# A fused encoder block on one core: the input's second half loaded behind row tile 1, modulation in two operations, the time steps inside the indexer, the feed-forward weight sums inside the top-k search

## The chip, the core and the metric

The kernel runs as one program on one core of one Trainium2 chip. The metric is the device time of one execution in microseconds (us). The engines are called PE (TensorE, matrix products; PEld is its weight load), DVE (VectorE), ACT (ScalarE), POOL (GpSimd) and SP (SyncE, which here only issues DMAs). Each engine works through its own list of instructions in order, and waits where the next instruction's inputs or buffers are not ready.

## The reference

One layer of a streaming encoder, over 1024 positions of width 1024, all in float32:

```python
mod = (silu(c) @ ada_w + ada_b)              # shift_m, scale_m, gate_m, shift_f, scale_f, gate_f
h = rmsnorm(x, pre_norm_mix) * (1 + scale_m) + shift_m
proj = h @ w_in      # q_lat, kv_lat, k_idx, w_idx, z, xbc, dt_raw, g_a, g_b
y_a = sparse_mla_attention(...) @ w_o_attn   # indexer scores -> top 256 keys per query -> attention
y_b = ssd_mixer(z, xbc, dt_raw, ...) @ w_o_ssd   # causal conv, dt = softplus(dt_raw + dt_bias), scan, silu(z) gate
mix = (sigmoid(g_a) * y_a + sigmoid(g_b) * y_b) @ w_out
x = x + gate_m * rmsnorm(mix, post_norm_mix)
h2 = rmsnorm(x, pre_norm_ffn) * (1 + scale_f) + shift_f
u_gate, u_up = split(h2 @ w_ffn_in)
x = x + gate_f * rmsnorm((silu(u_gate) * u_up) @ w_ffn_out, post_norm_ffn)
```

## The kernel before, in words

Activations lie transposed: 128 channels on the partitions, positions along the row, in two halves `b` = 0, 1 of 512 positions. The 1024 input channels are eight row tiles `k` of 128. Every float32 product is made of three PE products: each operand is split into a rounded part `hi` and a rest `lo`, and hi·hi, hi·lo and lo·hi are summed in PSUM.

**The head** (lines 345 to 501) makes `h`. PE's, ACT's and DVE's lists follow the written order there (`in_order`). For each row tile, `k_load` starts three DMAs on SP (the 192 KB piece `p1raw` of the first projection weight and two 512 KB pieces `ada` of the modulation weight), `k_ada` multiplies `ada` with the conditioning vector, `k_mod` finishes `amul` and `mod` (one scale and one shift per channel) and splits `p1raw`, `k_x` multiplies the half row tile by the spread reciprocal root `rx`, `k_h` makes `h`'s `hi` on ACT and `lo`, and `k_mm` runs its nine matmuls of 512 columns into the banks `pp`. `x_squares` and `rstd` make the norm's sums. The second half of `x` is eight DMAs of 256 KB from `x_load(1)`.

**The stages behind the head.** After `h` comes a run of wide projections: `wide` streams one 128-column tile of `w_in` and multiplies it with both halves of `h`, 48 matmuls, first into the bank of `b` = 0 and then that of `b` = 1, alternating over two pieces of four row tiles. These `pw` banks have three buffers in rotation (`bank_d`). Streamed weights are split by `whi` on ACT (L158) and `wlo` on POOL (L159). The fill list is

```python
FILL = "xxxxx" + "z" * 16 + "a" * 8
```

that is five conv groups of four tiles (evacuated by ACT and nine DVE operations, L1002 to L1004), sixteen `z` gates and eight `a` gates (evacuated by one ACT operation per bank, `g` at L992).

**What the fill stands beside.** The indexer makes scores with PE, ACT and DVE (`acc`, L667). Then the top-k search runs: two groups of rows in 32 dependent steps each. Group `v` counts on DVE (L715), group `s` counts on ACT (L717); both do their bookkeeping in DVE operations of 3 columns (L724 to L728, L757 to L760). ACT's list mixes the counts of `s` with the `g` evacuations of the fill. The time steps `dt` (`dt_part`, L567) are a chain of some seventeen DVE operations on 128x256 with a few small matmuls. `weight_sums` (L1022) makes sums and differences of blocks of `w_ffn_out`: in each of 12 units four loads, four POOL operations, four stores to the DRAM tile `d_t`, which the feed-forward output reads much later.

**What sets the order.** Outside the head a scheduler that walks its own timeline orders each engine's list when the program is built, bound by data, by buffers in rotation and by the `behind` dependences that the code adds. The order stays fixed when the program runs.

Of the kernel before, what the change touches and what calls it, by code (L numbers as in the profile page):

```python
# [17 lines left out]
P = 128  # L18
# [51 lines left out]
def build(tc, a, dbg=None, stop=99, slots=None):  # L70
# [23 lines left out]
    def f(x):  # L94
        return x.bitcast(F32)
# [251 lines left out]
    def x_load(b, after):  # L347
        for k in range(KT):
            t = Q(f"x{k}")
            tc.add_manual_dep(SP.dma_start(t, a["xT"][k][:, half(b)]).ins, after, mybir.DependencyInfo(  # L350
                mybir.DependencyClass.NoSync, mybir.DependencyReason.DATA), reason="behind")
            X0[k][b] = t

    def x_squares(b, ks, sums):
        for k in ks:
# [30 lines left out]
        first[k] = split(Q, raw, "p1", (P, 3, P), lo_eng=G)  # L386

    def k_x(k, b):
        V.tensor_tensor(X0[k][b], X0[k][b], rx[b], op=OP.mult)

    def k_h(k, b):
        x = X0[k][b]
        hi, lo = HB[b][k]
        i1 = S.activation(hi, x, AF.Identity, bias=mod[:, k:k + 1], scale=amul[:, k:k + 1])
        V.tensor_scalar(x, x, amul[:, k:k + 1], mod[:, k:k + 1], op0=OP.mult, op1=OP.add)
        i2 = (G if b and k > 1 else V).tensor_tensor(lo, x, f(hi), op=OP.subtract)
        if k == 7:
            barrier.update((i.ins.engine, i.ins.name) for i in (i1, i2))
        Hs[k][0][b], Hs[k][1][b] = hi, lo
        dump("h", x, (k, slice(None), half(b)))  # L400

    HB = [[(H_(f"h{k}h", dt=F32R), H_(f"h{k}l", dt=F32R)) for k in range(KT)] for b in BS]

# [15 lines left out]
    with in_order(*ORDERED):  # L419
        p = bank_d("warm")  # L420
        for i in range(WARM):
            T.matmul(p, ones, ones[:, None, :].to_broadcast([P, 4, P]), start=i == 0, stop=i == WARM - 1)
        sums = [None, None], [None, None]
        x_squares(0, range(2), sums[0])
        i = k_load(0, X0[1][0]).ins
        for k in (1, 2, 3):
            i = k_load(k, after=i.name).ins
        x_load(1, i.name)
        x_squares(0, range(2, 8), sums[0])
        r0 = rstd(sums[0], D)  # L430
        k_ada(0)
        pr0 = rspread(r0)
        k_mod(0)
        rx[0] = Q("rx")
        S.activation(rx[0], pr0, AF.Copy)
        pp1 = [[(bank if t or b else bank_d)(f"pp{t}") for b in BS] for t in range(3)]
        k_x(0, 0)
        k_h(0, 0)
        k_ada(1)
        k_x(1, 0)  # L440
        k_mm(0, 0, [0])
        k_mod(1)
        k_h(1, 0)
        k_mm(0, 0, [1, 2])
        k_ada(2)
        k_x(2, 0)
        k_mm(1, 0, [0])
        k_mod(2)
        k_h(2, 0)
        x_squares(1, range(2), sums[1])  # L450
        k_mm(1, 0, [1, 2])
        k_ada(3)
        k_x(3, 0)
        k_mm(2, 0, [0])
        k_mod(3)
        x_squares(1, range(2, 4), sums[1])
        k_h(3, 0)
        k_mm(2, 0, [1, 2])
        k_x(4, 0)
        x_squares(1, range(4, 8), sums[1])  # L460
        k_mm(3, 0, [0])
        k_load(4)
        k_ada(4)
        k_mm(3, 0, [1, 2])
        k_mod(4)
        k_h(4, 0)
        r1 = rstd(sums[1], D)
        k_mm(4, 0, [0, 1])
        pr1 = rspread(r1)
        rx[1] = Q("rx")  # L470
        S.activation(rx[1], pr1, AF.Copy)
        k_x(0, 1)
        k_h(0, 1)
        k_mm(4, 0, [2])
        i = k_load(5).ins
        barrier[i.engine] = i.name
        k_ada(5)
        k_x(1, 1)
        k_h(1, 1)
        k_x(2, 1)  # L480
        k_mm(0, 1)
        for k in range(5, KT):
            if k > 5:
                i = k_load(k).ins
                barrier[i.engine] = i.name
                k_ada(k)
            k_x(k, 0)
            k_mm(k - 4, 1, [0])
            k_mod(k)
            k_h(k, 0)  # L490
            k_mm(k - 4, 1, [1, 2])
            k_h(k - 3, 1)
            k_x(k - 2, 1)
            k_mm(k, 0)
        for k in range(5, KT):
            k_h(k, 1)
            if k + 1 < KT:
                k_x(k + 1, 1)
            k_mm(k - 1, 1)
        k_mm(KT - 1, 1)  # L500
        const_loads()
    if stop <= 0:
        ctx.close()
# [49 lines left out]
    kept = steady()  # L553
    dt, acum, decay, cdec = consts(kept)
    widx = kept[:, 896:1024].rearrange("p (t h) -> p t h", t=NT)
    tmp = [R("dt_tmp", (P, 4, NT, 32)) for _ in range(2)]
    xd, e, q, pl = (tmp[0][:, i] for i in range(4))
    dA = tmp[1][:, 0]
    for b in BS:
        pt = bank("pmt")  # L560
        for t in range(4):
# [5 lines left out]
    def dt_part():  # L567
        S.activation(e, xd, AF.Abs)
        i = S.activation(e, e, AF.Exp, scale=-1.0).ins.name
        nA = con.tile([P, 32], F32, name="nA")  # L570
        tc.add_manual_dep(S.activation(nA, alb, AF.Exp).ins, i, mybir.DependencyInfo(
            mybir.DependencyClass.NoSync, mybir.DependencyReason.DATA), reason="behind")
        V.tensor_scalar(q, e, 2.0, None, op0=OP.add)
        V.reciprocal(q, q)
        V.tensor_tensor(q, e, q, op=OP.mult)
        V.tensor_tensor(e, q, q, op=OP.mult)
        V.tensor_scalar(pl, e, 1.0 / 17.0, None, op0=OP.mult)
        for m in (15, 13, 11, 9, 7, 5, 3):
            V.scalar_tensor_tensor(pl, pl, 1.0 / m, e, op0=OP.add, op1=OP.mult)
# [12 lines left out]
        V.tensor_copy(acum.rearrange("p t h -> p (t h)"), pc[:, 0:256])
        tot = tmp[1][:, 1, 0:NCH, :]
        V.tensor_copy(tot.rearrange("p c h -> p (c h)"), ptot[:, 0:128])
        V.tensor_tensor(decay.rearrange("p (c t) h -> p c t h", t=2), tot[:, :, None, :].to_broadcast([P, NCH, 2, 32]),
                        acum.rearrange("p (c t) h -> p c t h", t=2), op=OP.subtract)
        S.activation(decay, decay, AF.Exp)
        S.activation(cdec, tot, AF.Exp)
        acT = [R("acT") for b in BS]
        for b in BS:  # L600
            pa = bank("pacT")
            for t in range(4):
                T.transpose(pa[0:32, t * P:(t + 1) * P], acum[:, 4 * b + t, :], ident)
            for dst, fn in ((d_ac, AF.Copy), (d_ea, AF.Exp)):
                t = acT[b][0:32, 512 * (fn == AF.Exp):512 * (fn == AF.Exp) + 512]
                S.activation(t, pa[0:32], fn)
                SP.dma_start(dst[2 * b:2 * b + 2].rearrange("c h l -> h c l"), t.rearrange("h (c l) -> h c l", c=2))
        dump("dt", dt)
        dump("acum", acum)
        SP.dma_start(d_kept, kept[:, 0:896])  # L610

    dt_part()


    bt = R("btmp", (P, 1024))
# [399 lines left out]
    KH = FT // 2  # L1015
    d_t = dr.tile([4, 4, P, KH, P], F32, name="d_t")
    units = iter([(c, k0) for c in range(4) for k0 in (0, 4, 8)])
    sum_bufs = [wp.tile([P, 4, P], F32, name="adaw", tag="adaw", bufs=2) for _ in range(2)]
    both = vp.tile([P, NT, P], F32, name="vt", bufs=1)
    sum_bufs += [both[:, 0:4], both[:, 4:8]]  # L1020

    def weight_sums(c, k0):  # L1022

        n = min(4, KH - k0)
        b11, b12, b21, b22 = (x[:, 0:n] for x in sum_bufs)
        for x, t, o in ((b11, c, 0), (b12, 4 + c, 0), (b22, 4 + c, KH), (b21, c, KH)):
# [41 lines left out]
    def conv_group(g):  # L1068
        for t in group_tiles(g):
            conv_out(conv(*t))  # L1070
            if g > 1:
                weight_sums(*next(units))

    pend = []

# [62 lines left out]
    for kind in FILL:  # L1138
        if kind == "x":
            conv_group(next(n_x))  # L1140
        elif kind == "z":
            t = next(n_z)
            gate(1 + t, d_z[t], AF.Silu)
            if t == 3:
                ada_after = [W.issue]
            if t == 12:
                rows.append(ada_rows())
        else:
            t = next(n_a)
            gate(49 + t, d_sga[t], AF.Tanh, 0.5)  # L1150
# [1084 lines left out]
```

## Time and profile before

| | |
|---|---|
| median of 3 runs | 2319.97 us (2319.41 to 2320.04) |
| profiled execution | 2321.74 us, of it the span from first to last instruction 2319.8 us |
| mean granted PE clock | 0.994 of full speed |
| PE busy | 2293.4 us, 99% of the span |
| DVE, ACT, POOL busy | 71%, 52%, 38% |
| DMA, mean over the span | 178 GB/s |

A matmul row shows its start, its duration and, in brackets, the idle time of its engine just ahead of it with what ended that idle time. Matmuls are pipelined: a row's duration is longer than the step to the next row (0.227 us at full clock, 0.427 us at half). In a group row the columns are line, engine, operation, output and inputs with shapes and count, then busy time, mean ns of one, and idle time ahead of the group. In a table of windows each engine has its busy time and the number of its instructions, then come the granted PE clock, the share of the 16 DMA engines in use, and GB/s.

### The profile page before, as it was taken

The numbers are of one execution on the slowest core, as the hardware profiler recorded it, in microseconds if no ns is written. First come the engines' busy times: TensorE is split into PE (matmuls) and PEld (weight loads), VectorE is DVE, ScalarE is ACT, GpSimd is POOL, SyncE is SP. The second block draws the span as 40 slices with busy tenths as digits, with TensorE's granted clock in tenths as the row PEclk, the third lists the DMA queues.
The fourth block names the chain that finished last, engine by engine and source line by source line (L and its number), as shares of the span: only waits on it lengthen the run. The fifth ranks groups of instructions, "written<-read, shape, count | busy, mean of one in ns | idle before, by whom it ended". The sixth has DMA issues, their size and how long they took to land. (4 is left out here: it accounts for less than half of the span.)

```text
span 2319.8 us, 34896 instructions
## 1 busy us (share of the span) xinstructions
PE 2293.4 (99%) x11672; PEld 1880.2 (81%) x11672; DVE 1650.2 (71%) x3249; ACT 1216.7 (52%) x2355; POOL 883.8 (38%) x691
## 2 busy tenths in 40 slices
PE   8999999999999999999999999999999999999997
PEld 5778888888888888888788788888788888888886
DVE  5466887399587777766567879685778776646675
ACT  4346666476635555556767666444555222235442
POOL 1434651222253334333335443100122555444556
PEclk8999999999999999999999999999999999999999
DMA  7137552522244444433679889674573444438664
GB/s 275 58 115 250 202 178 89 164 100 96 96 127 156 155 142 153 146 117 127 202 258 302 279 281 318 226 232 145 180 247 127 153 161 155 150 109 284 201 195 164
DMA packets 252147, 412.70 MB, mean 178 GB/s; under 512 B 25616, under 2 KB 93376, under 8 KB 251968
## 3 DMA queue, kind: packets, MB, share of 16 engines
q1 hardware_dynamic: 238720, 388.93, 50.8%
q10 hardware_dynamic: 13248, 21.56, 3.1%
q8 instruction: 92, 1.51, 0.3%
q14 instruction: 87, 0.71, 0.1%
HBM read 305.83 MB, written 107.70 MB: 178 GB/s over the span
## 5 line engine op out<-in xcount | busy, mean ns | idle before, releaser
L159 POOL TENSOR_TENSOR wlo<-wraw,whi 128x512 fp32r<-128x512 f32 x152 | 210.7, 1387 | 383.8 <-ACT whi L158 345.1
L1793 PE MATMUL p<-xh,wr 128*128 128x512 f32 x880 | 271.9, 389 | 0.0
L158 ACT ACTIVATE whi<-wraw 128x512 fp32r<-128x512 f32 x238 | 149.1, 628 | 204.7 <-issue 61.3
L1793 PEld LDWEIGHTS p<-xh,wr 128*128 128x128 f32 x880 | 165.2, 188 | 34.2
L1793 PE MATMUL p<-xl,wr 128*128 128x512 f32 x440 | 171.2, 389 | 0.0
L1787 POOL TENSOR_TENSOR wr<-a,wr 128x512 fp32r<-128x512 f32 x82 | 115.8, 1421 | 133.6 <-ACT wr L1786 100.0
L256 POOL TENSOR_TENSOR fwl<-fw,fwh 128x512 fp32r<-128x512 f32 (+1 forms) x78 | 106.3, 1371 | 103.9 <-ACT fwh L255 75.8
L872 ACT ACTIVATE lg<-lg,mx 128x256 f32<-128x256 f32 (+7 forms) x128 | 98.9, 773 | 74.8 <-DVE mx L869 74.1
L1786 ACT ACTIVATE wr<-a 128x512 fp32r<-128x512 f32 x107 | 66.7, 629 | 127.7 <-PE p L1793 89.5
L274 POOL TENSOR_TENSOR r<-v,nhalf 128x4 f32<-128x4 f32 (+1 forms) x17 | 25.4, 1497 | 255.1 <-DVE v L272 251.9
L667 DVE SCALAR_TENSOR_TENSOR acc<-rel,steady,acc 128x384 f32<-128x384 f32 (+2 forms) x90 | 103.1, 1175 | 13.6 <-ACT rel L662 13.5
L1793 PE MATMUL p<-h2h,wr 128*128 128x512 f32 x352 | 110.0, 390 | 0.0
L717 ACT ACTIVATE junk<-acc,cand__2214 128x1024 bf16<-128x1024 f32 (+2 forms) x96 | 86.2, 898 | 39.1 <-DVE cand__2214 L760 27.0
L662 ACT ACTIVATE rel<-prel 128x512 f32<-128x512 f32 (+3 forms) x160 | 77.2, 522 | 38.2 <-PE prel L661 36.6
L1793 PEld LDWEIGHTS p<-xl,wr 128*128 128x128 f32 x440 | 82.6, 188 | 17.2
L715 DVE TENSOR_SCALAR_CACHE_REDUCE junk<-acc,cand__2223 128x896 bf16<-128x896 f32 (+2 forms) x96 | 88.5, 922 | 1.4
L1717 PE MATMUL pos<-yh,wlo 128*128 128x512 f32 x224 | 87.8, 392 | 1.3 <-DVE wlo L159 1.3
L1717 PE MATMUL pos<-yh,whi 128*128 128x512 f32 x224 | 87.8, 392 | 0.0
L1717 PE MATMUL pos<-yw,whi 128*128 128x512 f32 x224 | 87.2, 390 | 0.0
L1787 POOL TENSOR_TENSOR wr<-s,wr 128x512 fp32r<-128x512 f32 x40 | 55.9, 1398 | 76.8 <-ACT wr L1786 69.5
L159 DVE TENSOR_TENSOR wlo<-wraw,whi 128x512 fp32r<-128x512 f32 x86 | 60.2, 701 | 34.1 <-ACT whi L158 33.9
L893 PE MATMUL pt<-ident,lg 128*128 128x128 f32 x576 | 82.8, 273 | 0.2 <-ACT lg L872 0.2
(691 smaller groups left out, 7279.0 us busy)
## 6 DMA issues: line engine op xcount, KB each, us to landing
wraw<-w_in SPq DMA_DIRECT2D x129, 256.0 KB, 2.7
a<-w_ffn_in SPq DMA_DIRECT2D x122, 256.0 KB, 3.3
al<-d_a SPq DMA_DIRECT2D x88, 256.0 KB, 4.2
yl<-d_y SPq DMA_DIRECT2D x72, 256.0 KB, 5.1
adaw<-ada_t SPq DMA_DIRECT2D x64, 256.0 KB, 2.7
al<-d_ac SPq DMA_DIRECT2D x32, 512.0 KB, 5.6
d_a<-g SPq DMA_DIRECT2D x42, 256.0 KB, 2.3
ada<-ada_p SPq DMA_DIRECT2D x16, 512.0 KB, 7.9
```

What stands on the lines that cost most here:

```text
L158: self.hi = behind(S.activation(hi[:, :kt], raw[:, :kt], AF.Copy))
L159: self.lo = behind(self.eng[len(self.tiles) % len(self.eng)].tensor_tensor(lo[:, :kt], raw[:, :kt], f(hi[:, :kt]), op=OP.subtract))
L256: (lo_eng or V).tensor_tensor(lo, src, f(hi), op=OP.subtract)
L662: S.activation(rel[:, 512 * b:512 * b + w_], pr[:, 0:w_], AF.Relu)
L667: V.scalar_tensor_tensor(acc[i][:, 0:n], rel[:, 0:n], ws, acc[i][:, 0:n], op0=OP.mult, op1=OP.add)
L715: V.tensor_scalar(jk, y, a_, 0.0, op0=op, op1=OP.add, accum_out=o)
L717: S.activation(jk, y, AF.Sign, scale=-1.0, bias=a_, accum_out=o)
L872: S.activation(lg[:, 0:n], lg[:, 0:n], AF.Exp, scale=-1.0, bias=m, accum_out=rr[:, 2 * t + hh:2 * t + hh + 1])
L893: T.transpose(ptv[:, hh, t, :], PR[hh, t][:, j * P:(j + 1) * P], ident)
L1717: T.matmul(p, w[k // 4][wi][:, k % 4], YO[i][k][xi], start=start and k == 0 and n == 0, stop=k == SK - 1 and n == 2, skip_group_check=True)
L1787: parts_last[0] = parts_eng[0].tensor_tensor(w[:, 1], src, f(w[:, 0]), op=OP.subtract).ins.name
L1793: T.matmul(p, w[:, wi, i], X[x][i][xi], start=start and i == 0 and k == 0, stop=i == 3 and k == 2, skip_group_check=True)
```

## The change

The change has four parts.

1. In the head, `x_load(1)` is issued behind the DMAs of row tile 1, not behind those of row tile 3; the loads of row tiles 4 to 7 are issued by a helper `k_more`; and the written order changes: the second half's squares and `rstd` come earlier, and from row tile 3 on both halves of a row tile are multiplied directly one after the other.
2. The modulation takes two operations behind `rx`: `k_x` multiplies by `amul` and `rx` in one DVE operation, ACT's `hi` then only adds `mod`, and `lo` is one DVE operation, (x + mod) - hi, for both halves. The DVE operation at L395 is gone, and POOL makes no `lo` of `h` any more.
3. `dt_part()` is called in the first `z` gate of the fill and not ahead of the indexer. Its temporaries lie in other buffers.
4. `weight_sums` is called in the `z` gates 4 to 15, one unit each, and not in the last three conv groups.

```diff
-        V.tensor_tensor(X0[k][b], X0[k][b], rx[b], op=OP.mult)
+        V.scalar_tensor_tensor(X0[k][b], X0[k][b], amul[:, k:k + 1], rx[b], op0=OP.mult, op1=OP.mult)
...
-        i1 = S.activation(hi, x, AF.Identity, bias=mod[:, k:k + 1], scale=amul[:, k:k + 1])
-        V.tensor_scalar(x, x, amul[:, k:k + 1], mod[:, k:k + 1], op0=OP.mult, op1=OP.add)
-        i2 = (G if b and k > 1 else V).tensor_tensor(lo, x, f(hi), op=OP.subtract)
+        i1 = S.activation(hi, x, AF.Identity, bias=m)
+        i2 = V.scalar_tensor_tensor(lo, x, m, f(hi), op0=OP.add, op1=OP.subtract)
...
-        for k in (1, 2, 3):
-            i = k_load(k, after=i.name).ins
-        x_load(1, i.name)
+        i = k_load(1, after=i.name).ins
+        i = x_load(1, i.name)
+        for k in (2, 3):
+            i = k_load(k, after=i).ins.name
...
+        for k in range(3, KT):
+            more = k + 1 < KT
+            if more:
+                k_ada(k + 1)
+            k_mm(k, 0, [0])
+            if more:
+                k_mod(k + 1)
+            k_mm(k, 0, [1, 2])
+            if more:
+                for b in BS:
+                    k_x(k + 1, b)
+                for b in BS:
+                    k_h(k + 1, b)
+            k_mm(k, 1)
...
-    dt_part()
...
             conv_out(conv(*t))
-            if g > 1:
-                weight_sums(*next(units))
...
             t = next(n_z)
+            if t == 0:
+                dt_part()
             gate(1 + t, d_z[t], AF.Silu)
+            if t > 3:
+                weight_sums(*next(units))
```

How the lists move is seen at three places. In the rows below a row has its line, the operation, output and inputs, the shape, and a count where it stands several times in a row; lines behind 350 have other numbers in the changed kernel.

SP's list at its start, before: `ada` are the modulation weights of one row tile, `x` with 128x512 the second half of the input.

```order
L368 DMA p1raw<-w_p 128x384
L373 DMA ada_198<-ada_p 128x1024
L373 DMA ada_199<-ada_p 128x1024
L368 DMA p1raw<-w_p 128x384
L373 DMA ada_204<-ada_p 128x1024
L373 DMA ada_205<-ada_p 128x1024
L368 DMA p1raw<-w_p 128x384
L373 DMA ada_210<-ada_p 128x1024
L373 DMA ada_211<-ada_p 128x1024
L350 DMA x_215<-xT 128x512
L350 DMA x_217<-xT 128x512
```

The same piece of SP's list in the changed kernel, from the weights of row tile 1 on:

```order
L375 DMA ada_198<-ada_p 128x1024
L375 DMA ada_199<-ada_p 128x1024
L350 DMA x_203<-xT 128x512
L350 DMA x_205<-xT 128x512
L350 DMA x_207<-xT 128x512
L350 DMA x_209<-xT 128x512
L350 DMA x_211<-xT 128x512
L350 DMA x_213<-xT 128x512
L350 DMA x_215<-xT 128x512
L350 DMA x_217<-xT 128x512
L370 DMA p1raw<-w_p 128x384
L375 DMA ada_220<-ada_p 128x1024
```

The eight `x` DMAs now stand ahead of the weights of row tiles 2 and 3.

DVE's list around the `dt` chain, before: `dt_tmp` are the chain's temporaries, `cv` with `pw` a conv tile's evacuation.

```order
L574 RECIPROCAL dt_tmp<-dt_tmp 128x256
L1002 SCALAR_TENSOR_TENSOR cv<-pw,vec,cv 128x511
L575 TENSOR_TENSOR dt_tmp<-dt_tmp 128x256
L576 TENSOR_TENSOR dt_tmp<-dt_tmp 128x256
L577 TENSOR_SCALAR dt_tmp<-dt_tmp 128x256
L579 SCALAR_TENSOR_TENSOR dt_tmp<-dt_tmp 128x256 x5
L1003 SCALAR_TENSOR_TENSOR cv<-pw,vec,cv 128x1
L1004 SCALAR_TENSOR_TENSOR cv<-pw,vec,cv 128x511
```

DVE's list around the chain in the changed kernel: `qs` and `acc` belong to the indexer.

```order
L642 TENSOR_TENSOR qs<-pqi,qs 64x256
L571 TENSOR_SCALAR dt_tmp<-dt_tmp 128x256
L572 RECIPROCAL dt_tmp<-dt_tmp 128x256
L998 SCALAR_TENSOR_TENSOR cv<-pw,vec,cv 128x1
L999 SCALAR_TENSOR_TENSOR cv<-pw,vec,cv 128x511
L997 SCALAR_TENSOR_TENSOR cv<-pw,vec,cv 128x510
L573 TENSOR_TENSOR dt_tmp<-dt_tmp 128x256
L998 SCALAR_TENSOR_TENSOR cv<-pw,vec,cv 128x2
L999 SCALAR_TENSOR_TENSOR cv<-pw,vec,cv 128x510
L642 TENSOR_TENSOR qs<-pqi,qs 64x512
```

The chain now begins behind the indexer's first rows and stands more thinly among the conv rows; it still is ahead of the search.

POOL's list from the last norm of the head to the end of the search, before: `wlo` is the split of a streamed weight, `nm` the first work of the attention.

```order
L274 TENSOR_TENSOR r<-v,nhalf 128x4
L256 TENSOR_TENSOR kvtl<-lat,kvth 128x512
L159 TENSOR_TENSOR wlo<-wraw,whi 128x512
L256 TENSOR_TENSOR kvtl<-lat,kvth 128x512
L159 TENSOR_TENSOR wlo<-wraw,whi 128x512 x41
L819 TENSOR_TENSOR nm<-nb,dmask 128x2x128
```

POOL's list within the search in the changed kernel: `adaw` and `vt` are the buffers of the weight sums (buffer numbers shown).

```order
L159 TENSOR_TENSOR wlo_4677<-wraw_4675,whi_4676 128x512
L1029 TENSOR_TENSOR vt_4735<-vt_4735 128x512
L159 TENSOR_TENSOR wlo_4754<-wraw_4752,whi_4753 128x512
L1026 TENSOR_TENSOR adaw_4736<-adaw_4737,adaw_4736 128x384
L1027 TENSOR_TENSOR adaw_4737<-vt_4735,adaw_4737 128x384
L1028 TENSOR_TENSOR vt_4735<-vt_4735,adaw_4736 128x384
L1029 TENSOR_TENSOR vt_4735<-vt_4735 128x384
L159 TENSOR_TENSOR wlo_4760<-wraw_4758,whi_4759 128x512
L159 TENSOR_TENSOR wlo_4834<-wraw_4832,whi_4833 128x512
L1026 TENSOR_TENSOR adaw_4736<-adaw_4737,adaw_4736 128x512
```

Where only `wlo` stood, each two `wlo` now have four sums beside them, in twelve units over the fill tiles `z` 4 to 15.

More of the change, by code (lines that the diff above doesn't have):

```diff
@@ L352, in x_load @@
             X0[k][b] = t
+            after = nc.cur_bb.bb.instructions[-1].name
+        return after
     def x_squares(b, ks, sums):
@@ L388, in k_x @@
     def k_x(k, b):
-        V.tensor_tensor(X0[k][b], X0[k][b], rx[b], op=OP.mult)
+        V.scalar_tensor_tensor(X0[k][b], X0[k][b], amul[:, k:k + 1], rx[b], op0=OP.mult, op1=OP.mult)
     def k_h(k, b):
-        x = X0[k][b]
+        x, m = X0[k][b], mod[:, k:k + 1]
         hi, lo = HB[b][k]
-        i1 = S.activation(hi, x, AF.Identity, bias=mod[:, k:k + 1], scale=amul[:, k:k + 1])
-        V.tensor_scalar(x, x, amul[:, k:k + 1], mod[:, k:k + 1], op0=OP.mult, op1=OP.add)
-        i2 = (G if b and k > 1 else V).tensor_tensor(lo, x, f(hi), op=OP.subtract)
+        i1 = S.activation(hi, x, AF.Identity, bias=m)
+        i2 = V.scalar_tensor_tensor(lo, x, m, f(hi), op0=OP.add, op1=OP.subtract)
         if k == 7:
@@ L399, in k_h @@
         Hs[k][0][b], Hs[k][1][b] = hi, lo
-        dump("h", x, (k, slice(None), half(b)))
     HB = [[(H_(f"h{k}h", dt=F32R), H_(f"h{k}l", dt=F32R)) for k in range(KT)] for b in BS]
@@ L425, in build, with k_more @@
         i = k_load(0, X0[1][0]).ins
-        for k in (1, 2, 3):
-            i = k_load(k, after=i.name).ins
-        x_load(1, i.name)
+        i = k_load(1, after=i.name).ins
+        i = x_load(1, i.name)
+        for k in (2, 3):
+            i = k_load(k, after=i).ins.name
         x_squares(0, range(2, 8), sums[0])
+        def k_more(k):
+            i = k_load(k).ins
+            barrier[i.engine] = i.name
         r0 = rstd(sums[0], D)
         k_ada(0)
+        k_more(4)
         pr0 = rspread(r0)
@@ L439, in build @@
         k_ada(1)
-        k_x(1, 0)
+        k_more(5)
         k_mm(0, 0, [0])
         k_mod(1)
+        k_x(1, 0)
         k_h(1, 0)
         k_mm(0, 0, [1, 2])
+        x_squares(1, range(4), sums[1])
         k_ada(2)
+        k_more(6)
+        k_mm(1, 0, [0])
+        x_squares(1, range(4, 8), sums[1])
+        k_mod(2)
         k_x(2, 0)
-        k_mm(1, 0, [0])
-        k_mod(2)
         k_h(2, 0)
-        x_squares(1, range(2), sums[1])
         k_mm(1, 0, [1, 2])
+        r1 = rstd(sums[1], D)
+        k_mm(2, 0, [0])
         k_ada(3)
[L453 to L468, printed above, removed]
+        k_more(7)
         pr1 = rspread(r1)
@@ L471, in build @@
         S.activation(rx[1], pr1, AF.Copy)
+        k_mm(2, 0, [1, 2])
         k_x(0, 1)
+        k_mod(3)
         k_h(0, 1)
[L474 to L477, printed above, removed]
         k_x(1, 1)
+        k_x(3, 0)
         k_h(1, 1)
+        k_h(3, 0)
+        k_mm(0, 1)
         k_x(2, 1)
[L481 to L500, printed above, removed]
+        k_x(3, 1)
+        k_h(2, 1)
+        k_h(3, 1)
+        k_mm(1, 1)
+        k_mm(2, 1)
+        for k in range(3, KT):
[12 more added lines that the diff above has]
+            k_mm(k, 1)
         const_loads()
@@ L555, in build @@
     widx = kept[:, 896:1024].rearrange("p (t h) -> p t h", t=NT)
-    tmp = [R("dt_tmp", (P, 4, NT, 32)) for _ in range(2)]
-    xd, e, q, pl = (tmp[0][:, i] for i in range(4))
-    dA = tmp[1][:, 0]
+    tmp = [wp.tile([P, 4, P], F32, name="dt_tmp", tag="adaw", bufs=2).rearrange("p (i t) (u h) -> p i (t u) h", i=2, h=32)
+           for _ in range(2)]
+    xd, e, q, pl = (x[:, i] for x in tmp for i in range(2))
+    dA = q
     for b in BS:
@@ L592, in dt_part @@
         V.tensor_copy(acum.rearrange("p t h -> p (t h)"), pc[:, 0:256])
-        tot = tmp[1][:, 1, 0:NCH, :]
+        tot = e[:, 0:NCH, :]
         V.tensor_copy(tot.rearrange("p c h -> p (c h)"), ptot[:, 0:128])
@@ L598, in dt_part @@
         S.activation(cdec, tot, AF.Exp)
-        acT = [R("acT") for b in BS]
         for b in BS:
@@ L604, in dt_part @@
             for dst, fn in ((d_ac, AF.Copy), (d_ea, AF.Exp)):
-                t = acT[b][0:32, 512 * (fn == AF.Exp):512 * (fn == AF.Exp) + 512]
+                t = EV("acT")[0:32]
                 S.activation(t, pa[0:32], fn)
@@ L1017, in build @@
     units = iter([(c, k0) for c in range(4) for k0 in (0, 4, 8)])
-    sum_bufs = [wp.tile([P, 4, P], F32, name="adaw", tag="adaw", bufs=2) for _ in range(2)]
-    both = vp.tile([P, NT, P], F32, name="vt", bufs=1)
-    sum_bufs += [both[:, 0:4], both[:, 4:8]]
+    sum_bufs = []
     def weight_sums(c, k0):
+        if not sum_bufs:
+            both = vp.tile([P, NT, P], F32, name="vt", bufs=1)
+            sum_bufs.extend([wp.tile([P, 4, P], F32, name="adaw", tag="adaw", bufs=2) for _ in range(2)]
+                            + [both[:, 0:4], both[:, 4:8]])
         n = min(4, KH - k0)
```

## The prediction

> **What bounds the kernel now.** I read the page's busy times first, then PE's waits, then the granted clock by windows, then the rows around the stretches that the change touches.
>
> The page's engines:
>
> ```profile
> PE 2293.4 (99%) x11672; PEld 1880.2 (81%) x11672; DVE 1650.2 (71%) x3249; ACT 1216.7 (52%) x2355; POOL 883.8 (38%) x691
> ```
>
> PE is busy for 2293.4 of 2319.8 us, and the change takes no matmul away. So time can only come from PE's waits and from stretches at half clock, and can only be lost by new ones. The waits of PE that concern us, in the whole span and then from 17 to 77 us alone (the head); columns: total us, times, longest:
>
> ```profile
> PE pw L235 <- DVE cv L1003: 1.9, 1, 1.9
> PE pw L235 <- ACT g L992: 0.4, 1, 0.4
> ```
>
> ```profile
> PE adap L305 <- DMA ada<-ada_p: 1.9, 2, 1.3
> PE pp L408 <- ACT h5h L394: 1.3, 1, 1.3
> PE pp L408 <- ACT h1h L394: 0.4, 1, 0.4
> PE pp L408 <- ACT h6h L394: 0.3, 1, 0.3
> ```
>
> The head's waits make 3.9 us. Windows (busy us of PE, PEld, DVE, ACT, POOL, then clock, DMA share, GB/s):
>
> ```profile
> 33.90:37.30 3.40, 2.85 (x25) 1.70 (x25) 2.22 (x4) 1.43 (x3) 0.57 (x1) 1.00 1.01 398
> 40.70:44.10 3.40, 3.20 (x17) 1.84 (x19) 0.69 (x1) 0.77 (x2) 0.67 (x1) 0.53 0.73 231
> 163.60:167.00 3.40, 1.49 (x7) 0.89 (x6) 3.40 (x6) 0.56 (x2) 3.17 (x4) 0.96 0.57 213
> 167.00:170.40 3.40, 3.40 (x10) 2.71 (x9) 3.17 (x6) 1.26 (x3) 1.19 (x1) 0.53 0.75 278
> 480.00:600.00 120.00, 120.00 (x531) 99.34 (x531) 113.17 (x398) 81.67 (x167) 27.33 (x21) 1.00 0.28 93
> ```
>
> A window in which PE worked 1.49 of 3.4 us is followed by one at clock 0.53; one with 2.85 is not. The last row is the search: PE never idles there, but DVE is busy for 113.17 of 120 us.
>
> **The time steps.** The one wait of 1.9 us, in PE's and DVE's timelines (start, duration):
>
> ```profile
> 164.23 0.39 PE L235 MATMUL pw<-h7h,wlo 128*128 128x512 f32 x1
> 166.53 0.63 PE L235 MATMUL pw<-h0h,whi 128*128 128x512 f32 x1 [1.91 <-DVE cv L1003]
> 170.28 0.39 PE L235 MATMUL pw<-h3h,whi 128*128 128x512 f32 x1
> ```
>
> ```profile
> 158.50 3.29 DVE L579 SCALAR_TENSOR_TENSOR dt_tmp<-dt_tmp 128x256 f32<-128x256 f32 x5
> 166.27 0.20 DVE L1003 SCALAR_TENSOR_TENSOR cv<-pw,vec,cv 128x3 f32<-128x3 f32 x1
> ```
>
> PE waits for the conv operation that frees a bank, and that operation stands behind the `dt` chain. From 164.23 to 170.28 PE issues ten matmuls; at the full-clock step (170.28 is followed by steps of 0.23) they would take 2.3 us, so 3.8 us are lost, wait and half clock together. The change pulls the chain apart and sets it beside the indexer's first heads, so this place goes: -3.8. But DVE now also has `qs` and `acc` rows there that PE's indexer products wait for. The trace of before has no such mixture; its bounds are nothing and the 3.8 of this same chain. I take +1.0, about half of the 1.91 wait without a half-clock stretch, since no five chain operations stand in one block ahead of a conv row any more. What is late next is a `qs` row or a conv bank behind the chain. Sum: -2.8.
>
> **The head.** Modulation per half row tile costs DVE one operation less:
>
> ```profile
> L389 DVE TENSOR_TENSOR x<-x,rx 128x512 f32<-128x512 f32 x16 | 13.7, 871 | 2.9 <-ACT rx L471 2.9
> L395 DVE TENSOR_SCALAR x<-x,amul,mod 128x512 f32<-128x512 f32 x16 | 8.7, 545 | 10.7 <-ACT h5h L394 1.8 <-ACT h6h L394 1.8 <-ACT h7h L394 1.8
> L1002 DVE SCALAR_TENSOR_TENSOR cv<-pw,vec,cv 128x509 f32<-128x509 f32 x12 | 8.8, 735 | 0.0
> ```
>
> Sixteen operations of 0.545 us go (8.7 us). The new fused ones have no row of their own; the nearest are 0.735 (a fused one from PSUM) and 0.871, so a row tile needs at most 4 x 0.87 = 3.5 us of DVE for both halves, against 18 matmuls of 0.227 = 4.1 us plus the modulation's products on PE. DVE keeps ahead, and I let the waits for `h` (1.3 + 0.4 + 0.3 = 2.0) go; ACT's `hi` is hidden beside the same matmuls, and if that cover is gone the 2.0 stay. Against it stands SP's queue. Row tile 2's weights are issued at 10.60 now, and land a median 7.9 us, at most 9.9 us, later:
>
> ```profile
> 10.60 1.91 SPq L373 DMA_DIRECT2D ada<-ada_p  x2
> DMA to landing us min/median/max: 3.8/7.9/9.9
> ```
>
> Eight DMAs of 256 KB are put ahead of them: 2.1 MB, 5.3 us at the 398 GB/s of the 33.9 window. So they land between 10.6 + 7.9 + 5.3 = 23.8 and 12.5 + 9.9 + 5.3 = 27.7; PE took them without a wait at 23.9 before, so it waits 0 to 3.8. I take 1.4, below the middle, because the second half's squares are there to fill some of it. The waits for row tile 4's weights (1.9) stay, as all earlier bytes are the same. The clock's half window at 40.7 moves with the gaps and is counted as unchanged. Sum: -2.0 + 1.4 = -0.6. Bounds: all 3.9 and the half window gone (3.4 x 0.47 = 1.6) is -5.5; a wait of 3.8 with one half window more and no wait gone is +5.4.
>
> **The weight sums in the search.** 48 POOL operations move there. In the indexer they cost PE nothing now (it has no wait there beyond 0.4 us), so leaving it gains nothing. In the search they meet DVE's small operations:
>
> ```profile
> 505.48 1.31 POOL L159 TENSOR_TENSOR wlo<-wraw,whi 128x512 fp32r<-128x512 f32 x1 [4.00 <-ACT whi L158]
> ```
>
> ```profile
> 505.56 1.25 DVE L760 TENSOR_TENSOR cand__2214<-ce__2213,c__2212 128x3 f32<-128x3 f32 x1
> ```
>
> An operation on three columns takes 1.25 us because a POOL operation is running; both end within 0.02 us of each other. Undisturbed ones take 0.16. How much that makes is seen from the groups of 434 to 610 us:
>
> ```profile
> L727 DVE TENSOR_TENSOR tm__2228<-tm__2228,cand__2223 128x3 f32<-128x3 f32 x32 | 7.4, 231 | 0.4
> L728 DVE TENSOR_TENSOR c__2221<-c__2221,tm__2228 128x3 f32<-128x3 f32 x32 | 7.2, 225 | 0.4
> L760 DVE TENSOR_TENSOR cand__2214<-ce__2213,c__2212 128x3 f32<-128x3 f32 x19 | 7.2, 378 | 0.1
> L724 DVE TENSOR_TENSOR tm__2228<-cnt__2224,kk__2225 128x3 f32<-128x3 f32 x32 | 6.6, 207 | 0.5
> L759 DVE TENSOR_SCALAR ce__2222<-ce__2222 128x3 f32<-128x3 f32 x23 | 6.2, 272 | 0.0
> L727 DVE TENSOR_TENSOR tm__2219<-tm__2219,cand__2214 128x3 f32<-128x3 f32 x27 | 6.2, 228 | 0.1
> L726 DVE TENSOR_TENSOR tm__2219<-cnt__2215,ks__2217 128x3 f32<-128x3 f32 x27 | 5.5, 205 | 21.8 <-ACT junk L717 21.4
> L760 DVE TENSOR_TENSOR cand__2223<-ce__2222,c__2221 128x3 f32<-128x3 f32 x23 | 4.8, 207 | 0.3
> ```
>
> ```profile
> L159 POOL TENSOR_TENSOR wlo<-wraw,whi 128x512 fp32r<-128x512 f32 x31 | 40.5, 1305 | 143.3 <-ACT whi L158 137.3 <-DMA nb<-d_skew 6.0
> ```
>
> The eight groups are busy 51.1 us; their 215 operations at 0.16 would be 34.4. The excess of 16.7 us over 31 POOL operations is 0.54 each. The bounds for a sum are 0 (it falls beside counts, which are not stretched) and 1.25 - 0.16 = 1.09. I keep 0.54.
>
> [...]
>
> Why this reaches PE: the `z` gates' banks are freed by `g` in ACT's list, between the counts of group `s`, and each step of `s` waits for DVE's small operations. PE's last matmul on a bank, and the `g` that frees it, early and late in the search:
>
> ```profile
> 474.60 0.39 PE L235 MATMUL pw<-h7h,wlo 128*128 128x512 f32 x1
> 605.16 0.39 PE L235 MATMUL pw<-h7h,wlo 128*128 128x512 f32 x1
> ```
>
> ```profile
> 475.03 0.60 ACT L992 ACTIVATE g<-pw 128x512 f32<-128x512 f32 x1
> 610.95 0.58 ACT L992 ACTIVATE g<-pw 128x512 f32<-128x512 f32 x1
> ```
>
> The lag grows from 0.0 to 5.4 us. With three banks in rotation PE can do 24 more matmuls (5.4 us) before it needs that bank, and indeed the 0.4 us wait for `g` in the list above follows. The slack is used up in the kernel before; more delay goes to PE in full. The changed order gives no new slack: between `g`s of a tile's first bank ACT counts 6.0 times on average before, 6.1 after. About 35 of the 48 sums fall where both groups search, the rest where only `s` is left and DVE has room. 35 x 0.54 = 18.9. DVE idles 6.8 of 120 us there, 5.7 in the 100 us concerned; I let half of it, 2.9, absorb delay, and 0.6 is left of the slack at that point: 18.9 - 2.9 - 0.6 = +15.4. Bounds: 0, and 35 x 1.09 - 3.5 = +34.7. The clock adds nothing if about 1.5 us of wait falls per `z` tile of 10.9 us; that lies between 0.55 and 1.91 idle of the windows above, so half clock is possible and lies in the upper bound.
>
> [...]
>
> The moved DMAs (4 loads and 4 stores a unit, on SP among the weight loads) meet a DMA share of 0.28 in the search, so bandwidth hides them; a store that waits for POOL could hold a weight load behind it, which the three-deep split buffers cover.
>
> **The sum.** -2.8 - 0.6 + 15.4 = +12.0 us. The profiled execution (2321.74) is 1.8 above the median, and the sum is set on the median: 2319.97 + 12.0 = 2332.0.
>
> **Rivals.**
> The search absorbs it: the sums fall beside the counts or into DVE's idle time. For it speaks that counts (L715) fill most of DVE's time and are not stretched; against it the 0.54 per `wlo`, measured at the same place. It decides where the cost per sum is under about (2.9 + 0.6) / 35 = 0.1. Then -2.8 - 0.6: 2316.6.
> The head gains all: no wait for weights, no half window, and the search absorbs too. -5.5 - 3.8 = -9.3: 2310.7. Against it stands the queue's 5.3 us.
> A small stall: 0.25 a sum (half of them meet counts), 8.8 - 3.5 = 5.3, less 3.4: 2321.9.
> The stall is dearer: chains of sums cost more the later in the chain, as POOL's rows in the indexer hint:
>
> ```profile
> L1029 POOL TENSOR_TENSOR adaw<-adaw 128x512 f32<-128x512 f32 x8 | 10.5, 1317 | 23.0 <-DMA adaw<-w_ffn_out 23.0
> L1031 POOL TENSOR_TENSOR vt<-vt,adaw 128x512 f32<-128x512 f32 x8 | 14.2, 1770 | 0.5
> ```
>
> The first of a chain takes 1.32 us, the third 1.77, held up by DVE. At 1.0 a sum: 35 - 3.5 - 3.4 = +28.1: 2348.
>
> **Chances.** The forecast 0.42, the dearer stall 0.12, the small stall 0.10, the search absorbs 0.25, the head gains all 0.11. A measurement of this kernel tells a change from none at about 0.2%, 4.6 us (2315.3 to 2324.6). "Absorbs" lies so near the lower line that I give 0.12 of it to faster and 0.13 to same; the small stall is same. Faster 0.23, same 0.23, slower 0.54. The range from 2311 to 2348 leaves out half of the first and last cases and the tails. The forecast's own range is 2325 to 2341.
>
> **What the profile after would show.** Right: POOL busy for about 8 of each 10.9 us of the search; 3-column DVE groups with means above 0.25; waits of PE for `g` of 10 us or more in all between 450 and 650; no wait for L1003 at 164; a wait for `ada` near 24 to 27 us. Wrong: no wait for `g`, and 3-column means as before. The forecast fails most easily at the 0.54, if POOL operations back to back do not cost what single ones do, and at the share of delay that DVE's idle time takes.

## The result, and the profile after

The changed kernel takes 2343.28 us (median of 4 runs, 2341.46 to 2346.59), the kernel before on the same chip 2319.69 us: a ratio of 1.0104 with a 95% interval from 1.0091 to 1.0116. It is slower by 23.6 us in the medians and by 19.9 us in the profiled spans (2339.7 against 2319.8). The forecast was 2332.0; its own range, 2325 to 2341, does not hold the measured time, the wide one, 2311 to 2348, does. Two single executions in the slow state, of 2842.95 us (the kernel before) and of 4641.17 us (the sums in the `a` gates), stand in none of the figures.

The page's engines and PE's one large wait after (total us, times, longest):

```profile
PE 2300.3 (98%) x11672; PEld 1885.5 (81%) x11672; DVE 1648.5 (70%) x3239; ACT 1211.0 (52%) x2353; POOL 851.5 (36%) x685
```

```profile
PE pw L235 <- ACT g L987: 16.1, 10, 3.1
```

The same number of matmuls; 0.4 us of waiting for `g` has become 16.1, in ten waits. Where the time went is seen at two marks that both kernels pass: the first `pmt` transposition behind the head, and the attention's first product `plg`. The work between them is the same but for four `pw` matmuls (0.9 us), which stand ahead of `pmt` before and behind it after. Of before, then of after:

```profile
147.17 0.38 PE L562 MATMUL pmt<-ident,lat 128*128 128x128 f32 x2
...
676.87 0.28 PE L860 MATMUL plg<-kvth,qh 128*128 128x256 f32 x1
```

```profile
144.81 0.38 PE L560 MATMUL pmt<-ident,lat 128*128 128x128 f32 x2
...
697.39 0.28 PE L855 MATMUL plg<-kvth,qh 128*128 128x256 f32 x1
```

At `pmt` the changed kernel is 2.4 us ahead (0.9 of it from the four matmuls), at `plg` 20.5 us behind, and it ends 19.9 behind. All the loss lies between the marks, and the windows show where (columns as before):

```profile
163.60:167.00 3.40, 3.40 (x17) 2.83 (x16) 3.30 (x6) 2.29 (x5) 1.56 (x1) 1.00 0.35 107
```

```profile
450.00:480.00 30.00, 26.52 (x116) 21.32 (x115) 29.23 (x78) 16.02 (x35) 17.45 (x15) 1.00 0.71 239
480.00:510.00 30.00, 29.27 (x121) 23.43 (x120) 28.79 (x98) 19.30 (x39) 15.56 (x13) 0.94 0.71 235
510.00:540.00 30.00, 26.86 (x107) 21.62 (x106) 29.51 (x82) 16.43 (x35) 19.45 (x18) 0.89 0.73 235
540.00:570.00 30.00, 25.55 (x111) 20.25 (x109) 29.34 (x87) 16.25 (x33) 15.91 (x13) 1.00 0.62 214
570.00:600.00 30.00, 26.73 (x104) 21.20 (x104) 19.23 (x58) 19.77 (x41) 10.23 (x9) 0.89 0.48 160
```

The hole at 164 us is gone: PE works through the window. In the search PE is no longer full, and in three windows it also ran below full clock: (0.06 + 0.11 + 0.11) x 30 = 8.4 us of clock that was not granted, beside 16.1 us of waiting. DVE stays at about 29 of 30 us until 570 us, and POOL's busy time in these windows has more than doubled.

One of the ten waits, in the rows of PE, ACT, DVE and POOL:

```profile
466.44 0.50 PE L235 MATMUL pw<-h0h,whi 128*128 128x512 f32 x1 [1.65 <-ACT g L987]
```

```profile
462.48 1.15 ACT L712 ACTIVATE junk<-acc,cand__2146 128x1024 bf16<-128x1024 f32 x1 [4.04 <-DVE tm__2160 L722]
...
465.81 0.58 ACT L987 ACTIVATE g<-pw 128x512 f32<-128x512 f32 x1
```

```profile
459.00 0.99 DVE L721 TENSOR_TENSOR tm__2151<-cnt__2147,ks__2149 128x3 f32<-128x3 f32 x1
...
460.72 0.38 DVE L722 TENSOR_TENSOR tm__2151<-tm__2151,cand__2146 128x3 f32<-128x3 f32 x1
...
461.69 0.50 DVE L723 TENSOR_TENSOR c__2144<-c__2144,tm__2151 128x3 f32<-128x3 f32 x1
```

```profile
458.97 1.01 POOL L1027 TENSOR_TENSOR adaw<-vt,adaw 128x384 f32<-128x384 f32 x1 [0.16 <-POOL adaw L1026]
460.06 1.02 POOL L1028 TENSOR_TENSOR vt<-vt,adaw 128x384 f32<-128x384 f32 x1
461.16 1.01 POOL L1029 TENSOR_TENSOR vt<-vt 128x384 f32<-128x384 f32 x1
```

PE waits for `g`; `g` stands in ACT's list behind three counts of group `s`, and ACT idles 4.0 us ahead of the first of them, until DVE has made the next candidate (the profile names the row just behind it). In the three DVE rows, which lead to that candidate, an operation of 0.16 us undisturbed (0.15 to 0.17 us for all 266 between 400 and 640 us of the kernel before that have no POOL operation beside them) ends within 0.03 us of the end of the sum beside it. The groups of DVE within 400 to 600 us, and two of POOL:

```profile
L722 DVE TENSOR_TENSOR tm__2160<-tm__2160,cand__2155 128x3 f32<-128x3 f32 x32 | 12.8, 399 | 0.5
L723 DVE TENSOR_TENSOR c__2153<-c__2153,tm__2160 128x3 f32<-128x3 f32 x32 | 10.3, 322 | 0.5
L719 DVE TENSOR_TENSOR tm__2160<-cnt__2156,kk__2157 128x3 f32<-128x3 f32 x32 | 9.2, 288 | 0.6
```

```profile
L1026 POOL TENSOR_TENSOR adaw<-adaw 128x512 f32<-128x512 f32 x8 | 10.4, 1294 | 22.0 <-DMA adaw<-w_ffn_out 21.9
L1029 POOL TENSOR_TENSOR vt<-vt 128x512 f32<-128x512 f32 x8 | 10.3, 1292 | 0.2
```

The same three groups had means of 231, 225 and 207 ns before. The sums on 512 columns take 1.29 us each at every place of the chain, those on 384 columns 1.01 to 1.05.

### The profile page after: what moved, and what is told of

Its sections match the earlier page's. It is cut to its first block, busy times and chain, and to the rows that moved or that the text cites. A ratio compares the mean times of both kernels' runs of the same rounds, so it can differ in the third digit from the quotient of the medians.

```text
span 2339.7 us, 34871 instructions
## 1 busy us (share of the span) xinstructions
PE 2300.3 (98%) x11672; PEld 1885.5 (81%) x11672; DVE 1648.5 (70%) x3239; ACT 1211.0 (52%) x2353; POOL 851.5 (36%) x685
## 4 chain that ended last, share of the span: by engine, by line
PE 68%; DVE 3%; DMA 1%; issue 1%; POOL 0%; ACT 0%; DVEq 0%
PE p L1792 18%; PE pw L245 9%; PE pfo L2057 8%; PE pos L1716 5%; PE plg L855 4%; PE poa L245 3%; PE pot L1504 3%; PE pw L235 3%; PE po L904 3%; PE pt L888 3%; PE puq L235 2%; PE pyd L1256 1%; PE pst L1261 1%; PE pyo L1266 1%; PE pyd L1257 1%
## 5 line engine op out<-in xcount | busy, mean ns | idle before, releaser
L662 DVE SCALAR_TENSOR_TENSOR acc<-rel,steady,acc 128x384 f32<-128x384 f32 (+2 forms) x90 | 84.8, 965 | 28.8 <-ACT rel L657 28.6
```

## The experiments

The theory: the sums' POOL operations in the search stretch DVE's three-column operations, so ACT's counts and with them `g` come late, PE waits and its clock halves. Rivals: the new order of indexer and search costs the time by itself; the sums' 96 DMAs on SP do; the `dt` chain does.

**The sums alone, in the kernel before.**

```diff
             conv_out(conv(*t))
-            if g > 1:
-                weight_sums(*next(units))
...
             gate(1 + t, d_z[t], AF.Silu)
+            if t > 3:
+                weight_sums(*next(units))
```

> The kernel before with nothing changed but the weight sums called in z gates 4 to 15. Theory: PE waits for g by 10 us or more and there are several windows at half clock in the search; slower than before by 20 to 27 us, 2340 to 2347. Rival 1 (it takes the new plan, with dt in the fill): below 2325. The stall at 164 us stays, since dt stands where it stood.

Measured: 2340.0 us, ratio 1.0090 (1.0075 to 1.0105), 21 us slower, with this wait:

```profile
PE pw L235 <- ACT g L992: 15.2, 7, 3.2
```

One part of the change on the list of before makes nearly the whole loss. The stall at 164 us shrank too, against the expectation: with the sums out of the conv groups its wait is 0.9 us, not 1.9, and no stretch at half clock follows.

```profile
PE pw L235 <- DVE cv L1003: 0.9, 1, 0.9
```

**The head alone.** The lines of the head as in the change, all else as before.

```diff
-        V.tensor_tensor(X0[k][b], X0[k][b], rx[b], op=OP.mult)
+        V.scalar_tensor_tensor(X0[k][b], X0[k][b], amul[:, k:k + 1], rx[b], op0=OP.mult, op1=OP.mult)
...
```

> The kernel before with the head of the changed one (the order of loads and of the written lists, and the modulation in two operations). Theory: the last pp matmul starts about 1.4 us earlier as in the changed kernel, and the whole is faster by 1 to 2.5 us, 2317 to 2319; the stall at 164 us stays. Rival (the head costs as much as it gains): 2319 to 2321.

Measured: 2321.72 us, ratio 1.0008 (0.9999 to 1.0018): no difference. The last `pp` matmul of the head starts at 73.9 us, 1.7 us ahead of before. Behind the head PE waits twice:

```profile
PE pcum L584 <- issue: 2.0, 1, 2.0
PE pw L235 <- DVE cv L1000: 2.0, 1, 2.0
```

The conv row still stands behind the `dt` chain (2.0 against 1.9 us), and the chain's own matmul now makes a second wait; neither is followed by a stretch at half clock here, so the two together cost about what the one stall did before. Compared by the number of matmuls done, PE is 1.8 us ahead when the kernel before stands at 408 us, and 0.6 at `plg`: what was gained in the head is mostly lost in the search.

**The sums back in the conv groups, with other buffers for `dt`.** The changed kernel without the two lines in the `z` gates, the two lines again in `conv_group`; the sums take the buffers first, so the `dt` temporaries need others:

```diff
-    tmp = [wp.tile([P, 4, P], F32, name="dt_tmp", tag="adaw", bufs=2).rearrange("p (i t) (u h) -> p i (t u) h", i=2, h=32)
+    tmp = [Q("dt_tmp").rearrange("p (i t h) -> p i t h", i=2, t=NT)
```

> The changed kernel with the weight sums called again in conv groups 2 to 4 (the dt temporaries lie in two other buffers of the same size, because the sums then hold the buffers first). Theory (the sums' POOL operations in the search stretch DVE's small operations, ACT's counts and so g come late, PE waits and halves its clock): no PE wait for g over 0.5 us in the search, time 2312 to 2316, about 28 us under the changed kernel. Rival 1 (the loss comes from the dt chain or from the new plan of indexer and search, whatever POOL does): still above 2330. Rival 2 (the head's gain and the 164 us stall are not real): about 2319.7, as before.

Measured: 2332.72 us, ratio 1.0059 (1.0044 to 1.0074). By these words the theory fell and the first rival stood. The trace shows another cause: PE's waits from 400 to 450 us are

```profile
PE pcum L585 <- DVE dt_tmp L581: 9.4, 1, 9.4
PE pw L235 <- ACT g L987: 2.7, 1, 2.7
```

With these buffers the scheduler had put the `dt` chain on DVE within the first steps of the search, where most of its operations stand behind a count, and PE's list reached the chain's product `pcum` 9.4 us too early. In the changed kernel the chain is ahead of the search and this wait doesn't exist. So this kernel did not undo one part; it added a new one.

**dt alone, with the same buffers.** The kernel before with `dt_part()` in the first `z` gate.

> The kernel before with only dt_part called in the first z gate (its temporaries in two other buffers). Theory: the wait at 164 us and its half-clock stretch go, no wait of more than 0.5 us comes in their place, the search is as before: faster by 3.5 to 4, 2315.7 to 2316.2. Rival (the chain beside the indexer's first heads makes a new wait): 2317 to 2321 with a PE wait for qs, rel or cv between 145 and 200 us.

Measured: 2344.61 us, ratio 1.0107 (1.0090 to 1.0124). Both sides missed it. It has the same 9.4 us, and a second stall in the head, which its own text does not touch:

```profile
PE pcum L588 <- DVE dt_tmp L584: 9.4, 1, 9.4
PE adap L314 <- ACT adaacc L308: 6.8, 1, 6.8
```

ACT's list had gained three small DMA issues in the head, between two squares that stand 10.9 us apart. It says nothing of `dt` alone; it shows how far a change of buffers moves work in this kernel.

**The sums back, with the chain kept in its place.** The `dt` temporaries in one buffer of another arena (a set of buffers that are used in rotation):

```diff
+    tmp = R("dt_tmp", (P, 1024)).rearrange("p (j i t h) -> p j i t h", j=2, i=2, t=NT)
+    tmp = [tmp[:, 0], tmp[:, 1]]
```

> The changed kernel with the weight sums back in conv groups 2 to 4, and the dt temporaries in one buffer of 1024 columns of the arena R, so that the dt chain stays ahead of the search (in the first such kernel it had moved into the search). Theory: only the sums in the search cost time; PE's waits for g are under 2 us and there is no wait for the dt chain: 2316 to 2320, about 25 us under the changed kernel, and within 3 us of the kernel before, since the kernel without sums was there too. Rival (the dt chain in the fill costs the search time by itself): 2325 or more.

Measured: 2317.91 us, ratio 0.9999 (0.9990 to 1.0007), the 25 us are gone. PE's only wait between 77 and 660 us:

```profile
PE pw L235 <- ACT g L987: 0.4, 1, 0.4
```

**The same with the changed kernel's lists up to the first sum**, two of the sums' buffers in the arena `EV`, which the evacuations use.

> The same, with the dt temporaries where the changed kernel has them and two of the sums' four buffers in the arena EV instead; every list keeps the changed kernel's order up to the first sum. Theory: 2316 to 2320 again. Rival: the sums, now holding two of nine buffers of the evacuations, make PE wait for conv evacuations in the indexer: 2321 to 2328.

Measured: 2323.94 us (2317.63 to 2326.57), ratio 1.0018 (1.0008 to 1.0028). The median lies in the rival's range, not in the theory's. The profiled execution has a span of 2315.8 us, so the trace at hand is its shortest execution and does not show what the median pays; whether the rival's cause makes it is left open. Most of the loss of the changed kernel is gone here too.

**The changed kernel without POOL's four operations** (loads and stores stay).

```diff
-        G.tensor_tensor(b11, b12, b11, op=OP.subtract)
...
-        G.tensor_tensor(b21, b22, b21, op=OP.subtract)
```

> The changed kernel with the four POOL operations of each weight-sum unit left out; the loads and stores stay, so d_t holds the unsummed blocks. Every other list keeps its order up to the search. Theory (POOL's operations hold up DVE's three-column operations): no PE wait for g over 1 us in all, no half-clock window in the search, 2314 to 2318. Rival (the 48 loads and 48 stores on SP's queue, or the new order of the indexer and search, cost the time): still over 2335.

Measured: 2320.79 us, ratio 1.0005 (0.9996 to 1.0015): 2.8 us above the range of the theory, far below the rival's, with waits for `g` of 1.6 us and no half clock in the search. **Half of them** (the first two of each unit):

> The changed kernel with the first two of each unit's four subtractions; the other two are left out (d_t holds wrong blocks), loads and stores stay. Theory (every reading POOL operation adds its share of delay, and no slack is left in the search): between the kernel without sums and the changed one, about half way: 2327 to 2335, with PE waits for g of 5 to 10 us. Rival (only the third and fourth of a chain, which the indexer's rows showed as the dearest, cost the time): 2319 to 2324.

Measured: 2329.62 us, ratio 1.0047 (1.0032 to 1.0062), with waits for `g` of 9.5 us. The windows from 450 to 630 us of the kernel before, without the four operations, with two of them, and with all four (the changed kernel):

```profile
450.00:630.00 180.00, 179.64 (x793) 148.43 (x792) 141.37 (x504) 126.55 (x258) 41.58 (x32) 1.00 0.29 97
```

```profile
450.00:630.00 180.00, 178.35 (x784) 146.55 (x783) 146.71 (x461) 113.21 (x229) 43.95 (x33) 1.00 0.61 203
```

```profile
450.00:630.00 180.00, 170.37 (x726) 137.27 (x725) 147.69 (x454) 111.73 (x229) 62.91 (x51) 0.98 0.60 199
```

```profile
450.00:630.00 180.00, 163.91 (x678) 131.14 (x677) 149.31 (x438) 107.26 (x220) 86.34 (x71) 0.95 0.60 199
```

The matmuls that PE gets through in 180 us fall from 784 to 726 to 678 with the POOL operations. The DMA share is 0.61, 0.60 and 0.60: transfers and SP's queue cost next to nothing. The new order of indexer and search costs nothing visible either (784 matmuls against 793, three waits for `g` of 1.6 us in all).

**POOL writing only.** The four subtractions replaced by four memsets of the same tiles:

```diff
-        G.tensor_tensor(b11, b12, b11, op=OP.subtract)
+        G.memset(b11, 0.0)
...
```

> The changed kernel with the four subtractions of each unit replaced by POOL memsets of the same tiles (the sums are zeros). POOL still works between loads and stores but reads nothing from SBUF. Theory as told by the rows so far (any POOL operation running beside a three-column DVE operation holds it until it ends): the time goes down only as far as the memsets are shorter than the 1.3 us of the sums. Theory of the shared read (only a POOL operation that reads holds DVE): excess on the three-column groups as in the kernel without sums, 2314 to 2318, whatever the memsets' length.

Measured: 2318.46 us, ratio 0.9995 (0.9985 to 1.0004). These memsets took 0.53 us on 512 columns, where the subtractions took 1.29, so POOL's time fell too, and the run doesn't part the two theories. **Ten memsets a unit** make POOL's time equal:

> The changed kernel with each unit's four subtractions replaced by ten POOL memsets of the same tiles (0.53 us each by the run with four memsets, so ten are 5.2 us against 5.2 us of the four subtractions). POOL is busy as long as in the changed kernel, but reads nothing. Theory of the shared read (only POOL operations that read SBUF hold DVE's three-column operations): the three-column groups as without sums, PE waits for g under 2 us, 2317 to 2322. Rival (POOL's time counts, whatever it does): PE waits of 10 us or more for g and 2335 to 2345.

Measured: 2328.65 us, ratio 1.0041 (1.0026 to 1.0055), waits for `g` of 9.5 us in four places: below what either side expected for the loss, above what the shared read gave. The rows of DVE, then POOL, show both at once:

```profile
481.23 0.16 DVE L722 TENSOR_TENSOR tm__2151<-tm__2151,cand__2146 128x3 f32<-128x3 f32 x1
481.31 0.15 DVE L722 TENSOR_TENSOR tm__2160<-tm__2160,cand__2155 128x3 f32<-128x3 f32 x1
...
482.96 3.52 DVE L754 TENSOR_SCALAR ce__2154<-ce__2154 128x3 f32<-128x3 f32 x1
```

```profile
480.35 1.58 POOL L1027 MEMSET adaw<- 128x512 f32 x3 [5.04 <-DMA adaw<-w_ffn_out]
481.89 1.30 POOL L159 TENSOR_TENSOR wlo<-wraw,whi 128x512 fp32r<-128x512 f32 x1
483.13 0.99 POOL L1027 MEMSET adaw<- 128x512 f32 x2
484.06 2.39 POOL L1027 MEMSET vt<- 128x512 f32 x5
```

Operations with two tensor inputs ran in 0.16 us in the middle of memsets here, so POOL's time alone does not hold them. Beside the subtractions, which read, 26 of the 56 such operations with nothing else of POOL beside them took longer than 0.2 us, up to 1.26 (changed kernel, 400 to 640 us). An operation with one tensor input and a scalar (L754) took 3.52 us beside memsets, through seven of them in a row. It is these operations that carry the loss of this kernel: between 400 and 640 us the 71 of them on three columns take 35.0 us, against 16.4 in the kernel without the four operations, the 241 with two inputs 60.1 against 53.6.

**The sums in the `a` gates, behind the search.**

```diff
-            if t > 3:
-                weight_sums(*next(units))
...
             gate(49 + t, d_sga[t], AF.Tanh, 0.5)
+            for _ in range(2 if t > 3 else 1):
+                weight_sums(*next(units))
```

> The changed kernel with the twelve units called in the eight a gates (one each in the first five, two or more in the last ones) and not in the z gates, so that they fall behind most of the search. Theory: PE's waits for g in the search go, what the change gains ahead of it (about 2 us in the head, 3.8 us at 164 us) stays: 2313 to 2317, faster than the kernel before. Rival (the sums then hold up the marking of the keys or the attention's first biases on DVE and POOL): 2318 to 2326 with a PE wait for plg or its inputs.

Measured: 2343.95 us, ratio 1.0113 (1.0096 to 1.0130). PE does not wait between 77 and 570 us, but its largest waits between 500 and 720 us are

```profile
PE pw L235 <- POOL wlo L159: 6.5, 6, 2.2
PE plg L855 <- DVE pc L891: 5.8, 1, 5.8
PE pw L235 <- ACT g L987: 5.1, 3, 2.3
```

Twelve units on eight tiles make POOL late for the weight splits that PE needs, and the attention starts late. The rival was right in kind, and its price was too low. **The same on the kernel before with the changed head:**

> The kernel before with the changed head and the weight sums in the a gates; dt_part stays ahead of the indexer. Theory: the sums cost nothing there, the wait at 164 us stays and is as long as in the kernel with the changed head alone: 2319 to 2323. Rival (taking POOL's sums out of the indexer shortens DVE's conv and dt operations, so that the wait at 164 us goes): 2314 to 2318.

Measured: 2353.13 us, ratio 1.0147 (1.0132 to 1.0162); both sides missed it for the same reason (waits of 7.4 us for `plg`, 7.1 for `g`, 6.9 for `wlo`).

No kernel run here beats the kernel before by more than its interval.

## Why the prediction was right, and which term was off

The direction and the mechanism came as forecast. The size did not: the forecast's own range missed, and 2343.28 lies nearer to the dearer stall's 2348 than to 2332.0.

**The search, +15.4.** The mechanism is shown: the loss goes with the sums in and out of the search (21 us for the sums alone, 25 us back when they are taken out), it follows the number of POOL operations (784, 726, 678 matmuls), and neither DMAs nor the order make it. The size of this term is what was off. Against the kernel without the four operations, whose lists on PE, ACT and DVE are the same, PE needs 24.1 us longer from the head's last `pp` to `plg`, where 15.4 was forecast. The step that was mis-sized is "about 35 of the 48 sums fall where both groups search": 46 of the 48 start before group `v`'s last small operation at 579.5 us. The price was nearly right: over all operations of three columns between 400 and 640 us the busy time rose from 70.1 us before to 99.6, so 29.5 us over 48 sums, 0.61 each, where 0.54 was taken. Of these 29.5 us, 24.1 reached PE; the slack and DVE's idle time were set at 3.5, and the difference says 5.4.

That PE's waits for `g` rose by 16.1 - 0.4 = 15.7 us, so near to 15.4, is luck: they are only part of the delay, as the clock shows.

**The clock, taken as nothing.** Stretches at half clock did come: 17.1 us in the search, with three of the waits (1.8, 3.1 and 3.0 us; two others, of 2.5 and 1.9 us, had none). That is 8.5 us of clock, and it looks like a term that was left out. But it took the place of further waiting. Four kernels with the same lists on PE, ACT and DVE show it:

| POOL in each unit | search, first to last count on ACT | PE, last `pp` to `plg` | waits for `g` | half clock |
|---|---|---|---|---|
| none | 181.2 us | 599.1 us | 1.6 us | 0 us |
| ten memsets | 194.0 | 611.9 | 9.5 | 10.2 |
| two subtractions | 194.5 | 612.4 | 9.5 | 6.8 |
| four subtractions | 205.4 | 623.2 | 16.1 | 17.1 |

PE loses what the search grows by, 12.7, 13.3 and 24.1 us, to within 0.1 us, however much of it is waiting and however much half clock. In each kernel PE's last wait for `g` comes at the search's end, behind the last stretch at half clock (at 621.8 us, behind 579.0, in the changed kernel). And PE's pace does not hold up the search: ACT waits for PE in it once,

```profile
ACT g L987 <- PE pw L235: 0.6, 1, 0.6
```

and once or twice for 0.6 us in the other three. So the prediction's "the clock adds nothing" held, but not for its reason, which was even waits between two idle times, 0.55 and 1.91 us. Such idle times do not settle it: the kernel with the head alone had two waits of 2.0 us and no half clock behind them.

**The time steps, -2.8.** The stall at 164 us went, and no new wait came between 77 and 450 us, so the +1.0 set against it was not needed. The gain is there: by the number of matmuls done, the changed kernel is 1.5 us ahead at the head's last `pp` and 6.7 us ahead when the kernel before stands at 408 us, so 4 to 5 us came between (the order of the matmuls differs in places, so this compares to about a microsecond). Not all of it belongs to `dt`: the sums alone, leaving the conv groups, made PE gain 2.6 us there, where the prediction gave nothing for that. Part of such a lead is lost again in the search, where `g` sets PE's pace: from 408 us to 633 us of the kernel before, the lead of the kernel without the four operations shrinks from 4.1 to 1.8 us and that of the kernel with the sums back from 5.2 to 3.8. That `dt` could stand badly was seen only by accident, in two kernels with other buffers (9.4 us).

**The head, -0.6.** The last `pp` matmul starts at 74.1 us against 75.6 before, 1.5 us ahead and within the bounds. But eleven profiled executions with the changed head put it between 73.3 and 76.8 us, two with the old head at 75.6 and 76.5 (and `dt` alone, with its stall there, at 84.6), so the gain is not clear of their spread. The two terms did not come as forecast: between 17 and 77 us the waits for `h` fell from 2.0 to 1.2 us, not to nothing, and those for weights fell from 1.9 to 0.9, where 1.4 more was set. The one for row tile 2 came where it was put:

```profile
25.23 1.08 PE L305 MATMUL adap<-ada,cs 128*32 128x256 f32 x8 [0.94 <-DMA ada<-ada_p]
```

**The account in the profiled executions.** PE is 6.7 us ahead at 408 us, 1.5 of it from the head; then 26.5 are lost in the search (24.1 by the sums, 2.4 that the kernel without them loses there too), and 0.1 behind it: +19.9.

**The rivals.** "The search absorbs it" and "a small stall" are refuted: PE's waits say so. "The dearer stall" (1.0 a sum) gave the nearest time and is refuted in its price, 0.61; its hint, that POOL's later rows in a chain take longer, did not carry over, since all four of a chain take the same time in the search (1.28 to 1.31 us on 512 columns). In the indexer of the kernel before the sums on 512 columns took 1.27 to 1.46 us where no `acc` operation of DVE (L667) ran beside them, and 1.75 to 2.16 us in 14 of the 16 cases where one did for about 1 us or more.

## What to carry to other kernels

An engine with idle time is not free room: where operations of two in-order engines hold each other up, ask whose small operations stand in a chain beside the new work, and follow that chain to the one buffer whose release PE needs. Look at the lag of a release along the whole stage, not at PE's waits: here PE was idle for 0.4 us in the search before, and the lag had just reached the last spare bank. Where a chain sets the pace, price how much longer the chain takes: the waits of the engine behind it undercounted that here (16.1 us of waits for 24.1 us of loss, with 17.1 us at half clock), and the clock was not to be added on top. For the same reason a lead won ahead of such a stage was partly lost in it (from 4.1 to 1.8 us in the kernel without the four operations). And an undo that moves buffers must have its order compared first, since it may undo something else.

## What the hardware showed that was not expected

A DVE operation on 3 columns with one tensor input took 3.52 us beside a row of seven POOL memsets of 0.53 us, where beside subtractions no three-column operation was held for longer than about one POOL operation (1.13 us more than its own time at most). It began beside a `wlo`, and ended with the last memset. The same came once more at 516.74 us (3.67 us, to the end of seven memsets), while the one at 515.16 took 0.23 us beside three; why is not shown. Of 90 two-input operations beside memsets alone, 86 took their 0.16 us.
